# The embedding gate's matrix product by seven block products over both token halves

## The chip, the cores and the metric

The kernel runs on one core of a Trainium2 chip. The metric is the device time of one execution in microseconds (us); the time before is the median of three runs. Beside it stands one profiled execution, from which all rows come. The engines are TensorE (PE, with PEld for its weight loads), VectorE (DVE), ScalarE (ACT), GpSimd (POOL), and the queues that start transfers, SP's and GpSimd's.

## The reference, cut to what matters

One decoder layer over 1024 tokens of width 2048, in float32. After the two attention groups the rest of the layer is:

```
h    = h + mixed @ w_out                                   # 2048 x 2048
gate = sigmoid(rmsnorm(h, norm_ple_g) @ w_ple_gate)        # 2048 x 2048
h    = h + gate * (p @ w_ple_proj)                         # 256 x 2048
out  = rmsnorm(h, norm_final_g)
```

where `rmsnorm(h, g)` divides each token's row by the root of its mean square (plus 1e-6) and multiplies by g. Since the division is one factor per token, it can be made after the product with the gate's weights; the kernel does so.

## The kernel before, in words

Everything is held transposed: 128 channels on the partitions, tokens along the free dimension. The 2048 channels are 16 chunks of 128, the tokens two halves of 512; half 1 (the earlier tokens, stored in reverse) is worked through first. Each float32 operand is split into a high part in the matmul's own format and a low part, what is left; a product of two operands is three matmuls (high by high, low by high, high by low). ScalarE makes the high part with a cast, VectorE the low part with a subtraction.

*The plain product* (`unit`) makes two output chunks for one half of the tokens: 4 pieces of weights, 8 input chunks by weight piece and output chunk, three matmuls each, 96 matmuls of 128x512 in all. The weights stream in 512 KB pieces through `wprep`, which casts and subtracts 1024 columns at once. The input projection and the embedding gate are made so; the gate reads its weights twice, once for each half of the tokens.

*The product by seven* (`class Seven`) takes a matrix product in 2 x 2 blocks, and makes it with seven block products instead of eight, in Winograd's form. One side of the blocks is the token half: rows 1 are half 1, rows 2 half 0. The operands of the seven products are A11, A12, A22 and the sums of rows S1 to S4 on one side, and B11, B21, B22 and the differences of weights T1 to T4 on the other. The V and gate columns of the input projection and the output projection are made this way. Each goes in two stages over the contraction: stage one covers eight of the 16 input chunks and stores half sums in DRAM, stage two covers the other eight, reads the half sums and adds them. A product for one pair of output chunks (`product`, L602 and on) is 4 chunks x 3 = 12 matmuls; an output pair is called u, from 0 to 7. Around each product, `prod` makes one high part (`whigh`) and one low part (`wlow`) of the weights three products ahead, and takes up to two pieces of other work from the queue `xq`, such as the splits of the next stage's operands. The table PLACE says which buffers hold the operands, WRING which buffers the weights' parts go through. A block's buffers come free when its last product of the stage is done; the loads of the next stage's operands are issued then and its splits two products later.

In the output projection (`op = Seven(...)`) the sums of rows S1 to S4 aren't made by VectorE: the attention writes and accumulates them in DRAM (`comb_d`) by transfers while it runs. Stage one writes half sums to `half_d` with plain stores; stage two adds them and accumulates the result by transfers into `h_d`, which holds x beforehand (`put`). At the end of stage two, `gate_loads` reads half 1's sixteen chunks of h back, scales them by `norm_ple_g` and splits them for the gate.

*The gate* then goes half by half. For half 1: eight units over the chunks of h; beside them the chunks of h are loaded once more (`load_h`), squared by ScalarE and summed by GpSimd (`SumSq`), which gives each token's mean square and its root after the third unit. `ple` makes the embedding's product (twelve matmuls for two output chunks), whose result ScalarE copies out of PSUM. `gated` multiplies the accumulator by the root, takes the sigmoid, multiplies by the embedding's product, adds to h, and squares the new h for the last norm. Half 0 follows in the same way, with its own loads, sums and splits. The last output pair of half 0 is made in two quarters of 256 tokens (`for tq`), each followed by the last norm (`final`) and the stores of the output.

The order on TensorE is the order written in the program throughout. In the output projection, and up to the gate's first two units, so are VectorE's and ScalarE's (`man2`); elsewhere a planner sets the order of those, and that of GpSimd and SP everywhere. On every engine instructions run strictly in their order.

## Time and profile before

| | us |
|---|---|
| median of the runs | 2490.62 (2489.23 to 2491.97, three runs) |
| the profiled execution | 2490.54 |
| its span | 2488.8 |
| TensorE busy | 2413.1 |
| VectorE busy | 1810.9 |
| ScalarE busy | 1201.2 |
| GpSimd busy | 280.1 |

The span is the time between the first and the last instruction of the profiled execution. A row of a group names the line of the kernel, the engine, the operation, what it writes and reads, its shapes and its count; behind that stand the busy time, the mean duration of one in ns, and the idle time before it with what ended it. A matmul's duration overlaps the next one's, so the pace is read from starts or from counts, not from durations.

### The profile page before, as it was taken

What the parts mean: (1) busy time and instruction counts of PE and PEld (TensorE: products, weight loads), DVE (VectorE), ACT (ScalarE), POOL (GpSimd) and SP (SyncE); (2) the same over time, 40 slices, a digit from 0 to 9 for tenths busy, and PEclk for the clock granted to TensorE, in tenths of its full rate; (3) what the DMA queues carried; (4) which work ended last, traced back from release to release, by engine and by line L of the source; (5) the groups of instructions that cost most, each with busy time, mean ns of one, the idle gap of its engine ahead of it and who ended that gap; (6) DMA issues with size and microseconds to landing.
All of it is one profiled execution on the core that took longest, in us unless ns stands there. A gap on an engine that the chain in (4) does not pass through costs nothing.

```text
span 2488.8 us, 31941 instructions
## 1 busy us (share of the span) xinstructions
PE 2413.1 (97%) x11434; PEld 2002.3 (80%) x11434; DVE 1810.9 (73%) x3010; ACT 1201.2 (48%) x2063; POOL 280.1 (11%) x361
## 2 busy tenths in 40 slices
PE   8999999999999999999999999998899999999997
PEld 6787878888888887888888888886787887787886
DVE  6788777778877778788888877877678674546555
ACT  5334335555555445565555555445423234546342
POOL 1211110000000000000000001110111113330110
PEclk9999999999999999999999999999999999999998
DMA  8776655444445556334444344555757777343433
GB/s 290 250 271 217 224 171 161 154 146 129 145 143 148 181 158 200 119 110 114 121 117 115 102 127 119 144 153 173 224 167 222 165 192 231 121 129 97 133 109 102
DMA packets 167471, 397.72 MB, mean 160 GB/s; under 512 B 18896, under 2 KB 23248, under 8 KB 167312
## 3 DMA queue, kind: packets, MB, share of 16 engines
q1 hardware_dynamic: 131040, 302.07, 37.7%
q0 software_dynamic: 36272, 93.60, 14.3%
q8 instruction: 90, 1.47, 0.2%
q14 instruction: 69, 0.57, 0.1%
HBM read 297.03 MB, written 106.95 MB: 162 GB/s over the span
## 4 chain that ended last, share of the span: by engine, by line
PE 82%; DVE 8%; DMA 4%; ACT 3%; issue 3%; SPq 0%; DVEq 0%; ACTq 0%
PE acc L232 17%; PE acc L233 17%; PE acc L234 17%; PE pbc L611 4%; PE pbc L609 4%; PE pbc L610 4%; PE tp L407 2%; PE z L311 1%; PE z L310 1%; PE pa L611 1%; PE pa L610 1%; PE pa L609 1%; PE av L454 1%; PE av L453 1%; PE av L452 1%
## 5 line engine op out<-in xcount | busy, mean ns | idle before, releaser
L232 PE MATMUL acc<-xh,whi 128*128 128x512 f32 x1568 | 629.0, 401 | 4.0 <-ACT xh L1070 2.5
L234 PE MATMUL acc<-xh,wlo 128*128 128x512 f32 x1568 | 613.8, 391 | 2.2 <-DVE wlo L154 2.2
L233 PE MATMUL acc<-xl,whi 128*128 128x512 f32 x1568 | 613.3, 391 | 0.3 <-DVE xl L1071 0.3
L154 DVE TENSOR_TENSOR wlo<-wraw,whi 128x1024 fp32r<-128x1024 f32 x252 | 312.1, 1239 | 193.3 <-ACT whi L153 187.6
L153 ACT CAST whi<-wraw 128x1024 fp32r<-128x1024 f32 x252 | 264.7, 1050 | 241.3 <-PE acc L233 214.9
L234 PEld LDWEIGHTS acc<-xh,wlo 128*128 128x128 f32 x1568 | 295.0, 188 | 67.5 <-DVE wlo L154 3.5
L232 PEld LDWEIGHTS acc<-xh,whi 128*128 128x128 f32 x1568 | 295.5, 188 | 59.2 <-ACT xh L1070 2.9
L233 PEld LDWEIGHTS acc<-xl,whi 128*128 128x128 f32 x1568 | 296.1, 189 | 54.8 <-DVE xl L1071 0.6
L699 ACT CAST wpr<-T 128x512 fp32r<-128x512 f32 x128 | 78.0, 621 | 317.3 <-DVE T L657 313.0
L426 ACT CAST awh<-tp 128x256 fp32r<-128x256 f32 (+1 forms) x160 | 80.8, 505 | 155.8 <-PE tp L407 155.8
L362 ACT ACTIVATE et<-z,mx 128x512 f32<-128x512 f32 (+7 forms) x128 | 94.8, 741 | 61.1 <-DVE mx L356 52.7
L115 POOL TENSOR_TENSOR ssq<-ssq,sq 128x512 f32<-128x512 f32 x56 | 83.9, 1500 | 304.5 <-ACT sq L114 253.8
L431 DVE TENSOR_TENSOR awl<-tp,awh 128x256 fp32r<-128x256 f32 (+1 forms) x160 | 92.2, 577 | 32.5 <-ACT awh L426 32.4
L356 DVE TENSOR_REDUCE mx<-z 128x1 f32<-128x512 f32 (+7 forms) x128 | 97.0, 758 | 4.4
L341 DVE TENSOR_TENSOR_SCAN st<-pt 128x511 f32<-128x511 f32 (+3 forms) x64 | 86.6, 1353 | 18.0 <-ACT pt L334 16.3
L713 DVE TENSOR_TENSOR wpr<-T,wpr 128x512 fp32r<-128x512 f32 x128 | 87.6, 685 | 6.4 <-ACT wpr L699 4.5
L609 PE MATMUL pbc<-cS,wpr 128*128 128x512 f32 x224 | 87.4, 390 | 3.2 <-DVE u L1485 1.6
L611 PE MATMUL pbc<-cS,wpr 128*128 128x512 f32 x224 | 87.2, 389 | 0.0
L610 PE MATMUL pbc<-cS,wpr 128*128 128x512 f32 x224 | 87.2, 389 | 0.0
L454 PE MATMUL av<-awl,v 128*128 128x256 f32 x256 | 73.8, 288 | 8.4 <-DVE awl L431 8.4
L334 ACT ACTIVATE pt<-z 128x512 f32<-128x512 f32 (+3 forms) x64 | 41.7, 651 | 78.8 <-DVE z L318 73.2
L232 PE MATMUL acc<-cA11h,whi 128*128 128x512 f32 x192 | 76.1, 396 | 0.0
(401 smaller groups left out, 5345.7 us busy)
## 6 DMA issues: line engine op xcount, KB each, us to landing
wraw<-w_in SPq DMA_DIRECT2D x192, 512.0 KB, 3.6
wraw<-w_gate SPq DMA_DIRECT2D x64, 512.0 KB, 3.6
wraw<-w_out SPq DMA_DIRECT2D x72, 256.0 KB, 3.7
wraw<-w_vg SPq DMA_DIRECT2D x71, 256.0 KB, 4.0
comb_d<-sg POOLq DMA_DIRECT2D x48, 256.0 KB, 7.4
spare<-xT SPq DMA_DIRECT2D x44, 256.0 KB, 4.1
xl<-h_d SPq DMA_DIRECT2D x40, 256.0 KB, 5.2
vghalf_d<-hc POOLq DMA_DIRECT2D x32, 256.0 KB, 4.1
```

Of the source, the lines that this page charges most:

```text
L153: side.later(1, lambda: A.copy(hi[:, o], raw[:, o]))
L154: side.later(side.wlo, lambda: V.tensor_tensor(lo[:, o], raw[:, o], hi[:, o].bitcast(F32), op=ALU.subtract))
L232: T.matmul(acc[c], hi[:, k2, kh, c, :], xh, start=first, stop=False)
L233: T.matmul(acc[c], hi[:, k2, kh, c, :], xl, start=False, stop=False)
L234: T.matmul(acc[c], lo[:, k2, kh, c, :], xh, start=False, stop=last)
L356: V.reduce_max(mx, z[:, vw], axis=AX.X, negate=True)
L362: A.activation(et[:, vw], z[:, vw], AF.Exp, bias=mx[:, 0:1], accum_out=l)
L431: V.tensor_tensor(wl[:, o, :], tp[:, o, :], wh[:, o, :].bitcast(F32), op=ALU.subtract)
L454: T.matmul(av, vv[:, 0, blk % 4, :], wl, start=False, stop=last)
L609: T.matmul(o, wh[:, w], xh, start=start and k == 0, stop=False, skip_group_check=True)
L610: T.matmul(o, wh[:, w], xl, start=False, stop=False, skip_group_check=True)
L611: T.matmul(o, wl[:, w], xh, start=False, stop=k == 3, skip_group_check=True)
```

## The change

The embedding gate becomes a third and fourth stage of the same object `op`, with `w_gate` laid out in blocks as `w_out` is. Its products, `Seven(..., 8, 4)`, run on directly behind the output projection's, with no change of weight streams.

- Stage one of the output projection now accumulates into `h_d` (which holds x); stage two reads `h_d` in place of `half_d`, adds, and stores h with plain stores. Two of its additions go from VectorE to GpSimd.
- In stage two, for each output pair u, ScalarE squares the four new chunks of h and GpSimd adds the squares, in pieces of 256 columns, into one sum for each half. VectorE makes the sums of rows S1 to S4 for the gate, scaled by `norm_ple_g` (`sums`), and SP stores them in `hcomb_d`.
- The gate's first stage (ph = 2) covers input chunks 0 to 3 and 8 to 11, its second (ph = 3) chunks 4 to 7 and 12 to 15. The first loads its operands as the output projection's last products free the buffers. The subtraction of four of these splits is GpSimd's. Both roots are made in the first stage.
- The second stage has only five of the seven products, those that half 1 needs. With them half 1 is finished: embedding product, sigmoid, addition to h, squares. What half 0 needs from them is added up and stored in `q_d`; the weight differences T3 and T4 that half 0 needs are stored in `tw_d`.
- A last pass of two products a unit (S3 by T3, A22 by T4) finishes half 0. In it the last norm of half 1 is made by GpSimd, in products of 1024 columns. Units 6 and 7 of the last pass are made in two quarters of 256 tokens at the end.
- The order of VectorE and ScalarE is the written one up to the end of the last pass's unit 5. `soon` holds steps that run one to three products later; up to three pieces of `xq` are taken behind a product when more than eight wait.

The diff, cut to its core:

```diff
-            def split(self, nm, i, hi, lo, gain=None, raw=None):
+            def split(self, nm, i, hi, lo, gain=None, raw=None, eng=V, apart=False):
...
+                def low():
+                    if gain is None:
+                        eng.tensor_tensor(lo, raw, hi.bitcast(F32), op=ALU.subtract)
+                    else:
+                        V.scalar_tensor_tensor(lo, raw, gain, hi.bitcast(F32), op0=ALU.mult, op1=ALU.subtract)
+                    self.XC[nm, i] = hi, lo
+
+                if apart:
+                    self.soon.append((self.slot + 1, low))
+                else:
+                    low()
...
+            def sources3(self, n, u, b22_):
+                def t2():
+                    self.diff("T1", "awh", self.B[12], self.B[11])
+                    self.wload(n + 1, 11)
+                    return self.diff("T2", "awl", b22_, self.T["T1"])
+                def t1():
+                    nc.sync.dma_start(tw_d[u][:, 0, :], self.diff("T3", "awh", self.B[12], b22_))
+                    self.wload(n + 1, 12)
+                    return self.t1
+                def b22():
+                    nc.sync.dma_start(tw_d[u][:, 1, :], self.diff("T4", "awl", self.B[21], self.T["T2"]))
+                    self.wload(n + 1, 21)
+                    return b22_
...
-                for _ in range(2):
+                for _ in range(3 if len(self.xq) > 8 else 2):
                     if self.xq and self.xq[0][0] <= self.slot:
                         self.xq.popleft()[1]()
...
-        op = Seven(lambda u, ph, k: ap["w_out"][u, ph, k], 8)
+        op = Seven(lambda u, ph, k: ap["w_out" if ph < 2 else "w_gate"][u, ph % 2, k], 8, 4)
+        tw_d = dram.tile([8, P, 2, HALF], F32, name="tw_d", tag="tw_d")
+        hcomb_d = dram.tile([4, 8, P, HALF], F32, name="hcomb_d", tag="hcomb_d")
+        q_d = dram.tile([8, 2, P, HALF], F32, name="q_d", tag="q_d")
...
+        class Squares:
...
+                elif self.wide:
+                    s = ev.tile([P, HALF], F32, name="s", tag="sq", bufs=2)
+                    A.activation(s, t, AF.Square)
+                    G.tensor_tensor(self.acc, self.acc, s, op=ALU.add)
+                else:
+                    for j in range(2):
+                        o = slice(j * 2 * P, j * 2 * P + 2 * P)
+                        s = ev.tile([P, 2 * P], F32, name="s", tag="sm", bufs=5)
+                        A.activation(s, t[:, o], AF.Square)
+                        G.tensor_tensor(self.acc[:, o], self.acc[:, o], s, op=ALU.add)
...
         def put(o, ph, hf, ch):
-            if ph:
+            if ph == 0:
                 G.dma_start(h_d[hf, ch], o, accum_op=ALU.add)
+            elif ph == 1:
+                G.dma_start(h_d[hf, ch], o)
+                ssh[hf].add(o)
             else:
                 G.dma_start(half_d[hf, ch], o)
...
+        def sums(u, hq, a2, b1):
...
+            def one():
+                A.activation(b2, b2, AF.Copy, scale=gb)
+                V.scalar_tensor_tensor(b2, a2, ga, b2, op0=ALU.mult, op1=ALU.add)
+                store("S1", b2)
+                V.tensor_tensor(a2, a2, a1, op=ALU.subtract)
+                store("S3", a2)
+            def two():
+                V.scalar_tensor_tensor(a1, a1, ma, b2, op0=ALU.mult, op1=ALU.add)
+                store("S2", a1)
+                V.scalar_tensor_tensor(b1, b1, mb, a1, op0=ALU.mult, op1=ALU.add)
+                store("S4", b1)
...
+        def gating(half, u, c, o, z):
+            V.tensor_tensor(o, o, rstd[half], op=ALU.mult)
+            def gate():
+                t = hpair[half, u][:, c, :]
+                V.tensor_tensor(o, o, z, op=ALU.mult)
+                V.tensor_tensor(t, t, o, op=ALU.add)
+            def squared():
+                t = hpair[half, u][:, c, :]
+                s2[half].add(t)
+                A.activation(t, t, AF.Copy, scale=gvec[:, 2, u + 8 * c:u + 8 * c + 1])
+            op.soon.extend([(op.slot + 1, lambda: A.activation(o, o, AF.Sigmoid)), (op.slot + 2, gate), (op.slot + 3, squared)])
...
+        begin(0)()
+        for u in range(6):
+            embedded = begin(u + 1) if u < 5 else None
+            prod(u, 4, "A22", bs[u], False)
+            q1, _ = qs.pop(u)
+            V.tensor_tensor(q1, bs[u], q1, op=ALU.add)
+            gating(0, u, 0, q1, zs[u])
+            if embedded:
+                embedded()
...
+            elif u > 2:
+                final(1, slice(0, HALF), s2[1].acc, {3: (4, 5), 4: (6, 7, 0), 5: (1, 2, 3)}[u], G)
...
-    a["w_gate"] = wsq(w_ple_gate)
+    a["w_gate"] = c(w_ple_gate[0].reshape(2, 2, 4, P, 2, 8, P).transpose(5, 1, 0, 3, 4, 2, 6).reshape(8, 2, 2, P, 2, 4 * P))
```

More of the change, by code (lines that the diff above doesn't have):

```diff
@@ L727, in prod @@
                 self.slot += 1
+                if u == 7 and len(self.units) == 32:
+                    for k in range(4):
+                        del self.XC[nm, k]
                 self.whigh()
@@ L1457, in rest_of, with embedding_load @@
             put(o, ph, hf, ch)
-        for ph in range(2):
+            if ph == 1:
+                hrows[u, hf] = o
+                if not first:
+                    xq.extend((op.slot + 1, fn) for fn in sums(u, hq, hrows.pop((u, 0)), hrows.pop((u, 1))))
+        praws = []
+        def embedding_load(half):
+            for k in range(2):
+                praw = ev.tile([P, HALF], F32, name="praw", tag="xt", bufs=4)
+                nc.sync.dma_start(praw, ap["pT"][k * P:(k + 1) * P, half * HALF:half * HALF + HALF])
+                praws.append(praw)
@@ L1499, in _body @@
                         rest_of(prev, False)
[L1500 to L1501 removed]
+                    p2()
                     prod(u, ph, "S1", c, True)
@@ L1651, in _body @@
[L1651 to L1662 removed]
+            b = {}
@@ new lines, in _body @@
+            ms = pp.tile([P, Q], F32, name="ssps", tag="t")
+            T.matmul(ms, ones, s2[0].acc[:, ts], start=True, stop=False)
+            for n, (u, c, o) in enumerate(os):
+                t = hpair[0, u][:, c, ts]
+                V.tensor_tensor(o, o, rstd[0][:, ts], op=ALU.mult)
+                sgi = A.activation(o, o, AF.Sigmoid)
+                V.tensor_tensor(o, o, z[u][:, c, ts], op=ALU.mult)
+                V.tensor_tensor(t, t, o, op=ALU.add)
+                s = ev.tile([P, Q], F32, name="sq", tag="sm", bufs=5)
+                if n < 3:
+                    A.activation(s, t, AF.Square)
+                else:
+                    V.tensor_tensor(s, t, t, op=ALU.mult)
+                T.matmul(ms, ones, s, start=False, stop=n == 3)
```

571 lines of the change are left out of this document (291 added, 280 removed).

## The prediction

> **What bounds the kernel now.** I read the page's busy times first, then the busy time of each engine by stretch, with the stretches laid at the seams between the stages, then what TensorE waited for.
>
> ```profile
> span 2488.8 us, 31941 instructions
> PE 2413.1 (97%) x11434; PEld 2002.3 (80%) x11434; DVE 1810.9 (73%) x3010; ACT 1201.2 (48%) x2063; POOL 280.1 (11%) x361
> ```
> ```profile
> core 0: us, PE busy (x) PEld busy (x) DVE busy (x) ACT busy (x) POOL busy (x), PEclk, DMA share, GB/s
> 1805.98:1898.57 92.59, 92.59 (x410) 76.62 (x408) 66.69 (x106) 26.56 (x47) 10.85 (x20) 1.00 0.55 184
> 1898.57:2051.58 153.01, 150.75 (x661) 123.39 (x660) 112.04 (x177) 46.44 (x83) 25.48 (x31) 1.00 0.76 187
> 2051.58:2071.06 19.48, 16.90 (x73) 13.36 (x72) 13.85 (x21) 9.68 (x16) 3.39 (x4) 1.00 1.01 276
> 2071.06:2258.68 187.62, 186.11 (x819) 153.47 (x818) 91.67 (x101) 99.51 (x140) 63.78 (x43) 1.00 0.44 144
> 2258.68:2300.49 41.81, 37.31 (x142) 27.87 (x140) 20.81 (x28) 22.82 (x29) 0.00 (x0) 0.92 0.32 100
> 2300.49:2447.37 146.88, 146.88 (x650) 121.66 (x649) 77.17 (x80) 58.90 (x79) 17.37 (x11) 1.00 0.36 117
> 2447.37:2489.00 41.63, 26.82 (x205) 25.13 (x203) 22.76 (x45) 11.42 (x18) 2.79 (x2) 0.83 0.31 102
> ```
>
> From the top: the output projection's first pass, its second pass, the seam to the gate, the gate of half 1, the seam between the halves, the gate of half 0, the end. TensorE is busy throughout; VectorE has 112 of 153 us in the second pass and half its time in the gate. So this part is bound by the number of matmuls, as long as the other engines keep up. Two stretches inside steady stages give the pace:
>
> ```profile
> 2300.49:2322.25 21.76, 21.76 (x98) 18.02 (x96) 11.64 (x14) 9.22 (x12) 1.82 (x1) 1.00 0.41 134
> 1939.98:1959.03 19.05, 19.05 (x86) 15.72 (x84) 12.86 (x20) 4.54 (x8) 3.42 (x4) 1.00 0.75 166
> ```
>
> The first is one unit of the gate, 96 weight loads and matmuls in 21.76 us: 0.2267 us per 128x512 matmul (two more matmuls only touch its edges). The second is one unit of the output projection's second pass, seven products of twelve, 2.72 us a product, 19.05 a unit; VectorE spends 20 instructions on it.
>
> **What is removed.** The plain gate takes 16 x 96 = 1536 matmuls of 512 columns (one unit as twice as many of 256). Seven products instead of eight take 1344. 192 x 0.2267 = 43.5 us go from TensorE; the program's order of instructions bears it out (146 fewer of 512 columns, 92 fewer of 256). With the plain gate go its own seams. Counting matmuls against stretches: 72 x 0.2267 = 16.3 of 19.48 us, so 3.2 lost at the seam to the gate; 816 x 0.2267 + 0.5 for the sums = 185.5 of 187.62, 2.1 lost in half 1; 132 x 0.2267 + 2.6 for the sums = 32.5 of 41.81, 9.3 lost between the halves. The waits name them:
>
> ```profile
> PE ple L1329 <- ACT ph L1301: 3.3, 2, 2.9
> PE pbc L609 <- DVE hc L1515: 2.5, 2, 1.8
> PE acc L232 <- DVE gt L1341: 1.5, 1, 1.5
> ```
>
> Together 14.6 us. The new order has no change of halves of that kind: both halves' rows are in each product, and rstd is ready in the gate's first pass. What takes their place is priced below, so I take all 14.6 off.
>
> **What is added, by the unit.** TensorE's order is fixed by hand and so is VectorE's and ScalarE's up to the last pass, so a stage goes at TensorE's pace or at VectorE's, whichever is longer. The durations:
>
> ```profile
> L713 DVE TENSOR_TENSOR wpr<-T,wpr 128x512 fp32r<-128x512 f32 x61 | 41.8, 685 | 0.9
> L115 POOL TENSOR_TENSOR ssq<-ssq,sq 128x512 f32<-128x512 f32 x56 | 83.9, 1500 | 304.5 <-ACT sq L114 253.8 <-ACT ssq L110 48.6
> 2192.20 2.68 POOL L115 TENSOR_TENSOR ssq<-ssq,sq 128x512 f32<-128x512 f32 x2 [7.61 <-ACT sq L114]
> 2145.22 0.68 DVE L1341 TENSOR_TENSOR gt<-zb,rstd 128x512 f32<-128x512 f32 x1
> 2145.82 0.68 DVE L1343 TENSOR_TENSOR gt<-gt,pls 128x512 f32<-128x512 f32 x1
> 2146.42 0.68 DVE L1341 TENSOR_TENSOR gt<-zb,rstd 128x512 f32<-128x512 f32 x1
> 2147.02 1.72 DVE L154 TENSOR_TENSOR wlo<-wraw,whi 128x1024 fp32r<-128x1024 f32 x1
> 2148.67 1.77 DVE L1344 TENSOR_TENSOR h<-h,gt 128x512 f32<-128x512 f32 x1
> 2146.32 3.58 POOL L115 TENSOR_TENSOR ssq<-ssq,sq 128x512 f32<-128x512 f32 x2 [25.11 <-ACT sq L114]
> ```
>
> VectorE's 512-column instructions start 0.60 us apart, so 0.61 each. GpSimd's addition of 512 columns takes 1.29 undisturbed (2.68 for two), 1.50 on average. The last rows are the dear ones: while GpSimd adds, VectorE's L1341, which reads one operand from PSUM, keeps 0.68, but L154 and L1344, both operands in SBUF, stretch, L1344 from 0.68 to 1.77. GpSimd's time is thus VectorE's time whenever VectorE's next instruction reads two operands from SBUF. The change raises GpSimd's additions from 56 of 512 columns to 47 of 512, 90 of 256 and 8 of 1024. For 256 I take half of 1.29, 0.65 (bounds: 0.65, and 1.29 if width did not matter); for 1024 twice, 2.58 (bounds 1.29 and 3.58).
>
> Output projection, second pass: 22 VectorE instructions (two additions go to GpSimd, four sums of rows come) = 13.4 us, GpSimd 2 x 1.29 + 8 x 0.65 = 7.8. Six of the 22 read PSUM, so 27% of GpSimd's time is covered: 13.4 + 0.73 x 7.8 = 19.1 against 19.05. At the edge: 0 to (13.4 + 7.8 - 19.05) x 8 = 17; I take 3 for unevenness.
>
> Seam to the gate: in two units VectorE issues 66 instructions (24 splits, eight sums among them), 40.3 us, and GpSimd 15.5 (four splits, twelve squares' additions, two others), 0.73 of it exposed: 51.6 against 2 x 19.05 = 38.1. 13.5 late; weights are prepared three products ahead, 8.2 us of lead. Lost 5.3 if the lead is whole, 13.5 if the pass before has eaten it: 9. The transfers crowd too: 28 operands, four rows, sums and weights are some 15 MB in 17 products (46 us), 326 GB/s, and today's seam in its fullest five, with the DMA share at 0.99, moved 327:
>
> ```profile
> 2045.00:2050.00 5.00, 5.00 (x24) 4.13 (x23) 4.91 (x8) 1.38 (x4) 0.84 (x1) 1.00 0.99 327
> ```
>
> They run beside the VectorE queue that is late anyhow; if not hidden, they alone would cost up to 5.
>
> Gate, first pass: 17 instructions, 10.4 of 19.05 us, GpSimd nearly idle: 0. Seam to its second pass: 36 instructions, 22.0 against 19.05, inside the lead: 1 (0 to 3). Second pass: five products and twelve embedding matmuls, 16.3 us a unit; 21 instructions, 12.8, and GpSimd 5.2, 71% exposed: 16.5. Eight units: 1.6, bounds 0 and (18.0 - 16.3) x 8 = 13.6; 2. Entry of the last pass: 33 instructions, 20.1 + 3.7 against 19.0, 4.8 late with some 3.7 of lead left: 3 (1 to 5).
>
> Last pass: two products and twelve embedding matmuls, 8.16 a unit; 11 instructions (6.7) and two additions at 64% (1.7) make 8.4. Into its second half fall the eight 1024-column products of half 1's norm, which were VectorE's: 8 x 2.58 = 20.6, 64% of it 13.2. Bounds 0 and 20; 10, a little slack taken off.
>
> The end. Today the last gate matmul starts at 2471.55 and VectorE's two quarters of the output are apart, the first under matmuls:
>
> ```profile
> 2471.55 0.28 PE L1650 MATMUL acq<-xh,wz 128*128 128x256 f32 x1
> 2479.16 4.30 DVE L1264 TENSOR_TENSOR h<-h,r 128x512 f32<-128x512 f32 x7
> 2483.38 0.87 DVE L1261 SCALAR_TENSOR_TENSOR h<-h,gvec,r 128x256 f32<-128x256 f32 x2
> 2468.30 16.57 SPq L1271 DMA_DIRECT2D out_dram<-h  x16
> ```
>
> In the new order both quarters stand behind the last matmul, and one more addition does: 5.2 more, covered in part by the second root's chain: 5 (0 to 10).
>
> TensorE's clock: after its longest wait (2.85) the matmuls started 0.43 apart for some microseconds, then 0.23 again, and that seam's row has the clock at 0.92; the seam to the gate, with waits up to 1.8, has it at 1.00.
>
> ```profile
> 2264.41 0.49 PE L1329 MATMUL ple<-ph,pwh 128*128 128x512 f32 x1 [2.85 <-ACT ph L1301]
> ```
> ```profile
> 2269.00 0.43 PE ple L1329
> 2273.97 0.23 PE acc L234
> ```
>
> The new stalls come in bits; one stretch of the first kind costs 0.08 x 41.8 = 3.3, none 0: I take 2. The Trainium skill (TensorE: Matmul & The Clock Gate, "What's actually happening") says the clock falls only after an idle window of about 3.4 us. By that the clock's term would be 0 and the sum 2 lower; the trace, with 2.9 us as its longest wait there and 0.43 behind it, is the harsher of the two.
>
> Costed at nothing, with their cover:
>
> ```profile
> L699 ACT CAST wpr<-T 128x512 fp32r<-128x512 f32 x61 | 37.3, 621 | 169.1 <-DVE T L657 169.1
> L1368 POOL DMA_DIRECT2D h_d<-hc x32 | 27.2, 852 | 123.0 <-DVE hc L1456 56.9 <-DVE hc L1515 47.6 <-DVE hc L1494 14.7
> L1370 POOL DMA_DIRECT2D half_d<-hc x25 | 13.6, 543 | 112.7 <-DVE hc L1456 72.8 <-DVE hc L1515 33.3 <-DVE wpr L713 5.2
> ```
>
> ScalarE has nine instructions of 0.62 and eight half as wide in a unit of the second pass, 9 of 19 us. The accumulating stores move from the second pass to the first: 32 x (0.85 - 0.54) = 10 us of GpSimd's issuing, into a stretch where it is busy 11 of 93 us and the DMA share is 0.55; uncovered, those 10 would be the price. SP's queue gets 140 more issues; a stored weight difference waits there for VectorE ahead of the next weight's load, covered by the three products of lead, and a bit of the 9 and 2 above if the lead is gone. Preparing the gate's weights twice in 1024-column pieces becomes preparing them once in 512-column pieces and differences; these are in the instruction counts above.
>
> Sum: 3 + 9 + 1 + 2 + 3 + 10 + 5 + 2 = 35 us of new losses. The profiled run took 2490.54, its span 2488.8, the median of the runs shown 2490.62, so one scale serves. 2490.5 - 43.5 - 14.6 + 35 = **2467.4**.
>
> **Rivals.** *Cover holds*: GpSimd's pieces fall into VectorE's gaps and the lead swallows the seams. For it: VectorE had 41 us free in the second pass. Against it: it has 5.6 of 19 us free now, and GpSimd wants 7.8. Left are the end (5), the entry (1), the seam (5) and unevenness (3): 2490.5 - 58.1 + 14 = 2446.
>
> *GpSimd takes VectorE's place as the bound* (the other side): nothing runs beside GpSimd's additions, because VectorE's queue nearly always has an instruction with two SBUF operands in front. Second pass 17, seam 13.5, 1024-column products 20, gate's second pass 13.6, entry 5, end 10, clock 3.3, gate's seam 3: 85, so 2490.5 - 58.1 + 85 = 2517. It decides from 58 us of losses on, that is when about 60% of the covered time isn't covered. For it L1344's 1.77; against it L1341's 0.68. The Trainium skill (SBUF — State Buffer, "Who interferes with whom") has this as an exclusive lock: whoever starts first keeps it for the whole instruction and the other blocks, and an instruction with at most one SBUF input is exempt. By that rule the trace's two kinds of rows are as they must be, and the six exempt instructions of 22 are all the cover there is.
>
> *The gain goes to transfers*, and the change doesn't do what it says: on top of the 35, 5 at each of three seams, and 1 in each of the last pass's six units, whose 1.8 MB in 8.16 us are 220 GB/s: 56, so 2488. For it the 0.99 above; against it the gate's 0.36 to 0.44.
>
> **How the numbers follow.** The forecast 0.50 (2452 to 2483), cover holds 0.23, GpSimd as the bound 0.18 (2497 to 2517), transfers 0.09 (five of the nine within 0.2%). A measurement of this kernel tells about 0.2%, 5 us, from no change. Faster: 0.50 + 0.23 + 0.04 = 0.77; same 0.06; slower 0.17. Range 2441 to 2504: below it a tenth, above it a tenth.
>
> **What would show it.** Gate matmuls still 0.2267 apart, a product 2.72. In the second pass, units of 19 to 20 us with VectorE near 95% busy, its two-operand rows averaging about 1.0 instead of 0.69 and waits of TensorE on `wpr`. At the seam a wait of TensorE of 5 to 13 us in all. In the last pass the eight 1024-column rows on GpSimd near 2.6 and VectorE's additions beside them above 2. I am wrong if VectorE's rows stay at 0.69 beside GpSimd, if units run over 21 us, or if TensorE waits for transfers rather than for VectorE.

## The result: 20 us slower

The changed kernel takes 2510.32 us (2510.15 to 2512.22), the kernel before 2490.91 beside it: a ratio of 1.008, with a 95% interval of 1.0063 to 1.0098. The prediction was 2467.4 with a range of 2441 to 2504. The profiled execution took 2510.15, its span 2508.4.

The head of the page of the changed kernel:

```profile
span 2508.4 us, 32433 instructions
PE 2390.8 (95%) x11198; PEld 1970.0 (79%) x11198; DVE 1965.9 (78%) x3251; ACT 1216.6 (48%) x2195; POOL 394.6 (16%) x498
```

TensorE has 22 us less busy time, GpSimd 115 and VectorE 155 more. The busy time of each engine by stretch, the stretches laid where TensorE starts a new pass (columns as in the prediction's table):

```profile
1906.84:2073.82 166.98, 159.04 (x673) 124.13 (x672) 140.75 (x189) 72.13 (x151) 87.12 (x101) 1.00 0.69 223
2073.82:2127.78 53.96, 44.68 (x169) 34.62 (x168) 46.62 (x61) 25.04 (x47) 19.24 (x20) 0.87 0.62 215
2127.78:2243.82 116.04, 116.04 (x509) 95.38 (x508) 72.64 (x112) 40.89 (x71) 12.96 (x24) 1.00 0.43 142
2243.82:2386.34 142.52, 136.41 (x589) 110.51 (x587) 126.54 (x177) 67.82 (x128) 53.29 (x58) 0.99 0.76 251
2386.34:2401.05 14.71, 10.27 (x39) 8.01 (x37) 14.61 (x22) 7.91 (x15) 4.25 (x5) 0.88 1.04 393
2401.05:2461.63 60.58, 47.61 (x195) 37.28 (x194) 57.16 (x59) 35.09 (x55) 35.91 (x19) 0.94 0.57 199
2461.63:2508.40 46.77, 27.54 (x140) 22.92 (x140) 34.74 (x73) 16.66 (x32) 5.49 (x4) 0.77 0.28 90
```

From the top: the output projection's second pass, the two units of the seam to the gate, the rest of the gate's first pass, its second pass, the entry of the last pass, the last pass, the two quarters with the end. What a stretch would take at TensorE's pace is the matmuls that the program has in it, by 0.2267 us (two of 256 columns count as one); what is above that is lost. Three rows are set beside the kernel before. It started the second pass at 1898.57; it took 153.0 us for 660 matmuls in that pass (149.6 at TensorE's pace, 3.4 lost); and it took 41.4 us, from 2447.37 on, for 96 matmuls and the end (21.8, 19.7 lost).

| stretch | taken | at TensorE's pace | lost | lost more than before | predicted (bounds) |
|---|---|---|---|---|---|
| up to the second pass | | | | 8.3 | 0 |
| second pass, 672 matmuls | 167.0 | 152.4 | 14.6 | 11.2 | 3 (0 to 17) |
| seam, 168 | 54.0 | 38.1 | 15.9 | 15.9 | 9 (5.3 to 13.5) |
| rest of the gate's first pass, 504 | 116.0 | 114.3 | 1.7 (two sums of squares) | 1.7 | 0 |
| gate's second pass, 587 | 142.5 | 133.1 | 9.4 | 9.4 | 1 + 2 (0 to 16.6) |
| entry of the last pass, 37 | 14.7 | 8.4 | 6.3 | 6.3 | 3 (1 to 5) |
| last pass, 192 and a sum of 1.1 | 60.6 | 44.6 | 16.0 | 16.0 | 10 (0 to 20) |
| the quarters and the end, 72 | 46.8 | 16.3 | 30.4 | 10.8 | 5 (0 to 10) |
| clock | | | | some 10, in the rows | 2 (0 to 3.3) |

The new losses add up to 79.6, against 35 in the prediction. The sums of squares that stand in no loss became 2.0 shorter (3.1 before, 1.1 now), so 2490.5 - 58.1 - 2.0 + 79.6 = 2510.0, and the profiled run took 2510.15. The saving of 58.1 thus came as reckoned, and the miss of 42.9 lies in the losses. What TensorE waited for from the second pass on, the four largest:

```profile
PE pa L616 <- DVE wpr L764: 13.5, 8, 4.4
PE pb L614 <- DVE qt L1749: 10.1, 3, 6.3
PE pbc L616 <- DVE wpr L764: 4.7, 7, 0.8
PE pbc L614 <- DVE hc L1683: 4.4, 1, 4.4
```

All four are VectorE: the weights' low parts (`wpr`) and accumulators it had not yet read. The next are shorter, among them 3.1 us for ScalarE's squares at the end and 2.4 for its casts of weights in the second pass. A steady unit of the second pass, and VectorE's own waits in it:

```profile
1967.37:1988.62 21.25, 20.09 (x85) 15.45 (x84) 17.12 (x23) 7.73 (x18) 11.74 (x15) 1.00 0.60 197
```
```profile
DVE wpr L764 <- ACT wpr L750: 1.5, 2, 0.8
DVE hc L1479 <- PE pbc L616: 1.4, 1, 1.4
DVE u L1551 <- PE pbc L616: 0.9, 1, 0.9
DVE hq L1458 <- ACT hq L1457: 0.8, 1, 0.8
```

The unit takes 21.25 in place of 19.05, and yet VectorE is busy for 17.12 of it only. It isn't full: it waits 4.6 us for TensorE and ScalarE, and TensorE then waits for it (0.8 us, and 0.4 for a cast that itself waits for VectorE). In the last pass GpSimd's rows and VectorE's beside them:

```profile
2433.00 22.36 POOL L1719 TENSOR_TENSOR h<-h,s2t 128x1024 f32<-128x1024 f32 x8
```
```profile
2436.33 0.68 DVE L1729 TENSOR_TENSOR qt<-pb,qt 128x512 f32<-128x512 f32 x1
2437.04 2.18 DVE L1618 TENSOR_TENSOR qt<-qt,ssh 128x512 f32<-128x512 f32 x1
2439.14 2.84 DVE L764 TENSOR_TENSOR wpr<-wraw,wpr 128x512 fp32r<-128x512 f32 x1
2441.90 0.68 DVE L1622 TENSOR_TENSOR qt<-qt,ple 128x512 f32<-128x512 f32 x1
```

With an operand in PSUM (`pb`, `ple`) an instruction keeps 0.68; with both in SBUF it takes 2.18 and 2.84, about the length of one of GpSimd's products (22.36 / 8 = 2.8).

### The profile page after: what moved, and what is told of

Read it like the earlier page. It is cut to its first block, busy times and chain, and to the rows that moved or that the text cites. A ratio compares the mean times of both kernels' runs of the same rounds, so it can differ in the third digit from the quotient of the medians.

```text
span 2508.4 us, 32433 instructions
## 1 busy us (share of the span) xinstructions
PE 2390.8 (95%) x11198; PEld 1970.0 (79%) x11198; DVE 1965.9 (78%) x3251; ACT 1216.6 (48%) x2195; POOL 394.6 (16%) x498
## 5 line engine op out<-in xcount | busy, mean ns | idle before, releaser
L227 PE MATMUL acc<-xh,whi 128*128 128x512 f32 x1152 | 466.2, 405 | 2.5 <-ACT xh L1136 2.5
L229 PE MATMUL acc<-xh,wlo 128*128 128x512 f32 x1152 | 452.3, 393 | 2.2 <-DVE wlo L154 2.2
L228 PE MATMUL acc<-xl,whi 128*128 128x512 f32 x1152 | 451.5, 392 | 0.3 <-DVE xl L1137 0.3
L154 DVE TENSOR_TENSOR wlo<-wraw,whi 128x1024 fp32r<-128x1024 f32 x192 | 234.1, 1220 | 48.5 <-ACT whi L153 47.1
L229 PEld LDWEIGHTS acc<-xh,wlo 128*128 128x128 f32 x1152 | 216.8, 188 | 51.2 <-DVE wlo L154 3.5
L227 PEld LDWEIGHTS acc<-xh,whi 128*128 128x128 f32 x1152 | 217.5, 189 | 40.7 <-ACT xh L1136 2.9
L228 PEld LDWEIGHTS acc<-xl,whi 128*128 128x128 f32 x1152 | 217.9, 189 | 38.1 <-DVE xl L1137 0.6
L614 PE MATMUL pbc<-cS,wpr 128*128 128x512 f32 x320 | 124.8, 390 | 3.2 <-DVE u L1551 1.6
L616 PE MATMUL pbc<-cS,wpr 128*128 128x512 f32 x320 | 124.5, 389 | 0.0
L615 PE MATMUL pbc<-cS,wpr 128*128 128x512 f32 x320 | 124.5, 389 | 0.0
L764 DVE TENSOR_TENSOR wpr<-wraw,wpr 128x512 fp32r<-128x512 f32 x80 | 77.3, 966 | 11.5 <-ACT wpr L750 11.5
L616 PE MATMUL pbc<-cS2h,wpr 128*128 128x512 f32 x176 | 71.8, 408 | 7.3 <-DVE wpr L764 7.3
```

Of the source, the lines that this page charges most:

```text
L154: side.later(side.wlo, lambda: V.tensor_tensor(lo[:, o], raw[:, o], hi[:, o].bitcast(F32), op=ALU.subtract))
L227: T.matmul(acc[c], hi[:, k2, kh, c, :], xh, start=first, stop=False)
L228: T.matmul(acc[c], hi[:, k2, kh, c, :], xl, start=False, stop=False)
L229: T.matmul(acc[c], lo[:, k2, kh, c, :], xh, start=False, stop=last)
L614: T.matmul(o, wh[:, w], xh, start=start and k == 0, stop=False, skip_group_check=True)
L615: T.matmul(o, wh[:, w], xl, start=False, stop=False, skip_group_check=True)
```

## The experiments

The theory going in: GpSimd's arithmetic on SBUF holds up VectorE's instructions with two SBUF operands, and through them TensorE. Unless another is named, the base is the changed kernel, 2510.32. The numbers in brackets are ratios to the kernel before with their 95% interval; the changed kernel's is 1.0063 to 1.0098, and the interval of an edit worth 5 us still touches it, so that such a difference is known to some 2 us.

### GpSimd's additions of the squares (second pass)

Left out (`adds` is False for the output projection's squares):

```diff
-                        G.tensor_tensor(self.acc[:, o], self.acc[:, o], s, op=ALU.add)
+                        if self.adds:
+                            G.tensor_tensor(self.acc[:, o], self.acc[:, o], s, op=ALU.add)
```

> The changed kernel, with GpSimd's additions of the squares in the output projection's second pass left out (92 or so of 256 columns; ScalarE still makes the squares, so the gate's root comes from one chunk alone and the numbers are wrong). Theory (GpSimd's additions hold up VectorE's instructions with two SBUF operands): the units of the second pass go from 21.25 us to 19.1 to 19.6, the pass from 167 to 155 or less, the seam to the gate gets 2 to 5 us shorter, and the whole 2510 comes to 2492 to 2498. Rival one (ScalarE's squares stand ahead of the weights' casts in its queue, and that chain is late): units of 20.7 or more, 2505 to 2510. Rival two (VectorE's own 22 instructions a unit, or the transfers, are the bound): no change, 2508 to 2512.

Given to VectorE:

```diff
+                        else:
+                            op.soon.append((op.slot + 1, partial(V.tensor_tensor, self.acc[:, o], self.acc[:, o], s, op=ALU.add)))
```

> The changed kernel, with the same additions of squares made by VectorE one product later in place of GpSimd: eight more instructions of 256 columns a unit on the engine that TensorE waits for. Theory (GpSimd's additions block VectorE): VectorE's unit is 13.4 + 8 x 0.4 = 16.6 us of unstretched work, under 19.05, so most of the gain of leaving the additions out stays: units of 19.3 to 20, the whole 2494 to 2503. Rival (VectorE's own instructions are the bound): each unit gets longer by the 3.2 us added, the whole 2520 to 2535.

Measured: 2490.88 without them (ratio to before 1.0005, 0.9994 to 1.0015), 2495.60 with VectorE making them (1.0020, 1.0010 to 1.0029). One unit, first without, then with them on VectorE:

```profile
1963.80:1982.97 19.17, 19.17 (x85) 15.71 (x84) 14.88 (x23) 7.74 (x18) 5.48 (x6) 1.00 0.67 220
```
```profile
1963.46:1982.81 19.35, 19.35 (x85) 15.63 (x84) 17.36 (x31) 7.74 (x18) 5.49 (x6) 1.00 0.66 215
```

The second pass comes from 167.0 to 154.1 and 155.2, the seam from 54.0 to 50.2 and 51.8. So the theory holds, and both rivals fall: ScalarE's squares are all still there, and more instructions on VectorE made the unit shorter. The three units say more than that. VectorE is busy 17.12 us with the additions on GpSimd and 17.36 with them on its own queue, and TensorE loses 2.2 us in the one and 0.3 in the other. It is not the amount of VectorE's time that GpSimd takes (17.12 - 14.88 = 2.2 of its 6.3 us of additions) but where it takes it: the first two rows below are the changed kernel's unit at its start, GpSimd's additions and VectorE's low part, for which TensorE waits; the third is the same instruction when VectorE makes the additions.

```profile
1966.86 1.43 POOL L1353 TENSOR_TENSOR ssh<-ssh,s 128x256 f32<-128x256 f32 x2
```
```profile
1967.35 1.50 DVE L764 TENSOR_TENSOR wpr<-wraw,wpr 128x512 fp32r<-128x512 f32 x1 [0.76 <-ACT wpr L750]
```
```profile
1963.13 0.69 DVE L764 TENSOR_TENSOR wpr<-wraw,wpr 128x512 fp32r<-128x512 f32 x1
```

TensorE's other wait in this unit goes back to GpSimd as well. Beside the next additions (from 1971.86) a difference of weights takes 1.94 in place of 0.69, ScalarE's cast waits for it, and TensorE for the cast:

```profile
1971.91 1.94 DVE L664 TENSOR_TENSOR T<-b,T 128x512 f32<-128x512 f32 x1
```
```profile
1973.89 0.62 ACT L750 CAST wpr<-T 128x512 fp32r<-128x512 f32 x1 [2.16 <-DVE T L664]
```
```profile
1974.56 0.50 PE L614 MATMUL pbc<-cS2h,wpr 128*128 128x512 f32 x1 [0.35 <-ACT wpr L750]
```

On VectorE's queue the additions stand behind the weights' low part and fill its waits; on GpSimd they run whenever a square is ready, and stretch what happens to be in front. The Trainium skill (SBUF — State Buffer, "Who interferes with whom") says that a VectorE instruction with at most one SBUF input, outside of the two-port modes, doesn't contend with GpSimd, and that issue order decides who blocks. The rows with 0.68 and 2.84 above agree with the first; no run here turns the order of issue alone around.

### All of GpSimd's arithmetic up to the last pass given to VectorE

```diff
-            return partial(op.split, nm, i, hi, lo, gain, None, G if ph == 2 and nm in ("S1", "S4") and i < 2 else V, ph > 0)
+            return partial(op.split, nm, i, hi, lo, gain, None, V, ph > 0)
```

> The changed kernel, with the four splits of the gate's first operands that GpSimd makes given to VectorE. Theory (GpSimd's SBUF work stretches VectorE's at the seam to the gate): VectorE does four more at 0.61, 2.4 us, and is freed of about two thirds of GpSimd's 7.6 us (2110 and 1719 ns each), so the seam gets 2 to 3 us shorter, the whole 2507 to 2509. Rival one (VectorE's count of instructions alone bounds the seam): 2.4 us longer, 2512 to 2514. Rival two (the transfers bound it): no change, within 1 us of 2510.

```diff
-                    G.tensor_tensor(u2, u2, r[1, u + 8], op=ALU.add)
+                    V.tensor_tensor(u2, u2, r[1, u + 8], op=ALU.add)
...   (s1, q1 and q2 likewise, all squares' additions, and the splits as above)
```

> The changed kernel, with every arithmetic instruction of GpSimd up to the last pass given to VectorE: the squares' additions one product later, the additions of half sums, the sums for half 0 and the four splits. Theory (GpSimd costs VectorE more than its work is worth): units of the output projection's second pass 19.05 to 19.5, the seam 2 us shorter, units of the gate's second pass 16.3 to 16.7 in place of 17.45, so 2510 less 15, 2.5 and 5: 2485 to 2490, at or a little under the kernel before. Rival (VectorE is then the bound itself, with 13.4 + 1.2 + 3.2 = 17.8 us of instructions in a unit of 19.05 and about 15.6 in one of 16.3, and no room for unevenness): units of 20 and 17.5, 2497 to 2508.

Measured: 2508.76 for the splits alone (inside the range expected, but with a seam of 54.8, no shorter), 2496.39 for all (1.0023, 1.0015 to 1.0031). No gain over the squares alone: units of 19.56, seven units of the gate's second pass 122.1 in place of 123.9. The second theory fails here, and its rival is nearer. VectorE was now busy 18.29 of 19.56 in a unit:

```profile
1968.72:1988.28 19.56, 19.44 (x85) 15.61 (x84) 18.29 (x33) 7.74 (x18) 2.16 (x4) 1.00 0.65 213
```

So giving work back paid while VectorE had waits to fill; with 18.29 of 19.56 it gained nothing more.

### The seam: VectorE or the transfers

Ten low parts left out (`skip` is true in the gate's first pass for the last two chunks of A11, S2, A12, S1 and S4):

```diff
                 def low():
-                    if gain is None:
+                    if skip:
+                        pass
+                    elif gain is None:
```

> The changed kernel, with ten of VectorE's low-part subtractions at the seam to the gate left out (the last two chunks of A11, S2, A12, S1 and S4; the matmuls then read the unsplit row as its own low part, so the numbers are wrong; transfers, casts and matmuls stay). Theory (the seam is bound by VectorE's count of instructions, whoever else reads SBUF): ten at 0.7 us go, and the two units of the seam come from 54 us to 47 to 49, the whole 2503 to 2505. Rival (the transfers bound it, their share is 0.9 to 1.0 there at some 320 GB/s): no change, 2509 to 2511.

Measured: 2505.61 (1.0058, 1.0043 to 1.0073), the seam 48.1. The first of its two units, in the changed kernel and with the ten left out:

```profile
2073.82:2101.31 27.49, 22.64 (x85) 17.19 (x83) 27.28 (x35) 16.64 (x33) 13.37 (x14) 0.88 0.80 278
```
```profile
2075.31:2098.60 23.29, 21.25 (x86) 16.75 (x84) 23.12 (x29) 16.83 (x33) 13.03 (x14) 0.93 0.93 340
```

VectorE is busy from end to end in both, and the unit is as much shorter as its busy time; the transfers, moving 340 GB/s in place of 278, had had room. So in the first unit it is VectorE's count, as the theory had it. In the second VectorE is busy for 19.33 of 26.47; TensorE's one long wait there, 4.4 us, is again for a low part, which stands behind two splits that take 3.43 beside two of GpSimd's (3.40). TensorE's waits for low parts are 9.0 of the seam's 15.9. Most of the rest is the clock, 0.87 in its row: behind each of the two long waits some twelve matmuls start 0.43 us apart in place of 0.23, 5 us in all. The first of them:

```profile
2078.62 0.80 PE L616 MATMUL pa<-cA11h,wpr 128*128 128x512 f32 x1 [4.18 <-DVE wpr L764]
2079.21 0.63 PE L614 MATMUL pa<-cA11h,wpr 128*128 128x512 f32 x1
2079.64 0.63 PE L615 MATMUL pa<-cA11l,wpr 128*128 128x512 f32 x1
```

So it is after all four waits over 4 us (4.18, 4.43, 4.44, 6.32). After one of 2.62 in the last pass the matmuls kept their pace, but after one of 2.45 at the entry to the gate's second pass they did not:

```profile
2430.62 0.50 PE L614 MATMUL pb<-cS3h,wpr 128*128 128x512 f32 x1 [2.62 <-DVE qt L1749]
2430.95 0.40 PE L615 MATMUL pb<-cS3l,wpr 128*128 128x512 f32 x1
2431.19 0.39 PE L616 MATMUL pb<-cS3h,wpr 128*128 128x512 f32 x1
```
```profile
2251.88 0.80 PE L614 MATMUL pbc<-cA,wpr 128*128 128x512 f32 x1 [2.45 <-DVE hc L1479]
2252.47 0.63 PE L615 MATMUL pbc<-cA,wpr 128*128 128x512 f32 x1
2252.89 0.63 PE L616 MATMUL pbc<-cA,wpr 128*128 128x512 f32 x1
```

The same wait (2.45 and 2.46) was followed by some five matmuls at full pace and then 0.43 in the run without the squares' additions, and by full pace throughout in the version put together below. Over the five places of the changed kernel, up to the end of the last pass, the slow matmuls cost some 10 us. The Trainium skill (TensorE: Matmul & The Clock Gate, "What's actually happening") puts the fall behind an idle window of about 3.4 us. The waits over 4 us and the one of 2.62 agree with it; the 2.45 does not, nor does the 2.85 of the kernel before, shown in the prediction, where three waits under 1 us came between it and the 0.43. What decides between 2.4 and 2.9 us, no run here shows.

### The last pass

Half 1's norm on VectorE, and left out on either:

```diff
-                final(1, slice(0, HALF), s2[1].acc, {3: (4, 5), 4: (6, 7, 0), 5: (1, 2, 3)}[u], G)
+                final(1, slice(0, HALF), s2[1].acc, {3: (4, 5), 4: (6, 7, 0), 5: (1, 2, 3)}[u], V)
```

> The changed kernel, with the eight products of 1024 columns that make half 1's last norm given back to VectorE. Theory (they block VectorE's SBUF instructions for most of their 22.6 us): VectorE's own eight take some 1.2 us each, 9.6 in all, against 22.6 x 0.64 = 14 blocked, so the last pass gets 4 to 8 us shorter, the whole 2502 to 2506. Rival (GpSimd's products run beside VectorE's work and the last pass is late by VectorE's own instructions): the 9.6 us are added, less a little slack, 2514 to 2520.

```diff
-                    eng.tensor_tensor(t, t, r.unsqueeze(1).to_broadcast([P, 2, ts.stop - ts.start]), op=ALU.mult)
+                    if half == 0:
+                        eng.tensor_tensor(t, t, r.unsqueeze(1).to_broadcast([P, 2, ts.stop - ts.start]), op=ALU.mult)
```

> The changed kernel, with the eight products of 1024 columns of half 1's last norm left out (its rows are stored without the factor, the transfers stay). It gives the whole price of those products in the last pass, which came out the same on either engine. Theory (on GpSimd they block VectorE for most of their 22.6 us): the last pass is 10 to 14 us shorter, the whole 2496 to 2500. Rival (the last pass is late by VectorE's own order, a chain through the sigmoid and the weights' casts, and the products fill its gaps): 0 to 4 us, 2506 to 2510.

The squares' additions left out as well:

```diff
-                    G.tensor_tensor(self.acc, self.acc, s, op=ALU.add)
+                    if not self.wide:
+                        G.tensor_tensor(self.acc, self.acc, s, op=ALU.add)
```

> As the run before it, and GpSimd's additions of half 0's squares in the last pass left out too (its last norm is then made from one chunk's squares), so that GpSimd does no arithmetic behind the last pass's entry. Theory: the units of the last pass come down to 8.16 to 8.5 us and only the entry's loss is left, the whole 3 to 6 us below the run before it, 2491 to 2496. Rival (VectorE's own instructions bound the pass): units of 9 or more and no further gain, within 2 us of the run before it.

Measured: 2510.84 on VectorE, 2505.52 without the norm (1.0059, 1.0046 to 1.0072), 2497.09 without both (1.0031, 1.0021 to 1.0040). With the norm on VectorE the whole did not change, though the last pass itself came to 55.7 in place of 60.6: the end took 51.6 in place of 46.8. The rows stretched by GpSimd's products were gone, but the products stood two or three in a row ahead of the weights, and VectorE once waited 3.6 us behind them for a load of h; six of the eight products now stood in the end's stretch. Without the norm the pass took 56.1; the whole fell by 4.8, between the theory's 10 to 14 and the rival's 0 to 4. Left out after it, the eleven 512-column additions gave more than the eight products of twice the width, 8.4 us against the 3 to 6 expected: 4.9 in the pass (51.2 left) and most of the rest at the end. The units didn't come down to the 8.5 expected. 51.2 is still 6.6 above TensorE's pace without any of GpSimd's arithmetic, so 9.4 of the 16.0 lost went with GpSimd's. What shows in the rest is a late transfer: ScalarE's cast of a weight difference waits for it, and VectorE waits 4.3 us behind the casts (that run's order of time on ScalarE, and VectorE's waits from 2400 to 2451):

```profile
2411.30 0.62 ACT L750 CAST wpr<-wraw 128x512 fp32r<-128x512 f32 x1 [6.99 <-DMA wraw<-tw_d]
```
```profile
DVE pwhl L1517 <- ACT pwhl L1516: 4.9, 2, 4.3
```

### Transfers at the entry of the last pass

```diff
-                qs[u + 2] = load_q(u + 2)
+                with tc.issue_after(q1i.ins): qs[u + 2] = load_q(u + 2)
```

> The changed kernel, with the last pass's loads of half 0's stored sums held back until the unit two before has been added up, in place of running ahead as buffers allow (same transfers, same order). Theory (at the entry of the last pass, where the transfers move 390 GB/s for 35 us, ScalarE's and VectorE's queues wait for weights behind these loads: 5.35 us for tw_d, 3.2 for w_pp): those waits shrink by half, the last pass is 2 to 4 us shorter, the whole 2506 to 2508. Rival (the waits are hidden by what VectorE is late with anyway): within 1 us of 2510.

```diff
-                kt = PLACE["A12" if u < 4 else "S4"][u % 4][1]
+                kt = PLACE["A12"][u % 3][1]
```

> The changed kernel, with the buffers for half 0's stored sums cut from sixteen to six (three units), so that their loads wait for a buffer and are spread over the last pass; the hold tried before had not moved a single load. Theory (at the entry of the last pass the weights' transfers stand behind these loads): ScalarE's wait of 5.35 us for tw_d falls under 3, the last pass is 2 to 4 us shorter, the whole 2506 to 2508. Rival (what is late there is VectorE and the chain of two weight buffers): within 1 us of 2510.

The first edit moved no load (seven of them were issued in a row at 2396, as without it), so its 2510.50 tells nothing of transfers; it repeats the changed kernel, with every stage the same within 0.7 us. The second gave 2507.09 (1.0063, 1.0050 to 1.0076): ScalarE's wait for `tw_d` went from 7.2 in all to 0.4, its wait for the embedding's weights from 3.2 to 5.1, and the last pass with its entry got 1.1 shorter, the end 2.2. None of its four runs is as slow as one of the unedited kernel's, but the intervals overlap. Some 1 to 3 us may be the transfers'; that isn't settled.

### The accumulating stores

```diff
-                G.dma_start(h_d[hf, ch], o, accum_op=ALU.add)
+                G.dma_start(h_d[hf, ch], o)
```

> The changed kernel, with the first pass's stores into h_d made plain in place of accumulating (the residual x is left out of the result, nothing else changes: same transfers, same queue, same order). The second pass starts at 1906.8 after the change, at 1898.6 before it. Theory (the accumulating stores, moved to the first pass, cost those 8 us, by GpSimd's issuing and by reading back what they add to): the second pass starts 5 to 8 us earlier, the whole 2502 to 2506. Rival (the 8 us come from the order of loads at the end of attention or of the added ones, not from these stores): less than 2 us, 2508 to 2512.

The same part alone, in the kernel before:

```diff
             if ph:
-                G.dma_start(h_d[hf, ch], o, accum_op=ALU.add)
+                G.dma_start(h_d[hf, ch], o)
             else:
-                G.dma_start(half_d[hf, ch], o)
+                G.dma_start(h_d[hf, ch], o, accum_op=ALU.add)
...
-                    nc.sync.dma_start(r[e], half_d[e])
+                    nc.sync.dma_start(r[e], h_d[e])
```

> The kernel before, with one part of the change alone: the output projection's first pass accumulates into h_d and its second pass reads that back, adds and stores plainly (same result, same number of transfers). Theory (the accumulating stores at the end of attention and in the first pass are what the first pass lost): the second pass starts 4 to 7 us later than the 1898.6 of the kernel before, the whole 2494 to 2498. Rival (they hide there as the prediction had it, GpSimd's issuing only): within 2 us of 2491.

Only the eight stores made while attention runs, plain:

```diff
-                put(o, 0, 1, u + i)
+                G.dma_start(h_d[1, u + i], o)
```

> The changed kernel, with only the eight stores into h_d made while attention still runs plain, the other 24 of the first pass accumulating as in the change (x is missing from these eight chunks). Theory (the accumulating stores cost at the seam into the first pass, where the transfers' share is 1.0): most of the 5.7 us that all 32 gave come back, 2505 to 2507. Rival (the cost lies in the steady first pass, by the 24): less than 1.5 us, 2508.5 to 2511.

Measured: 2504.62 with all plain (5.7 less than the changed kernel; 1.0063, 1.0046 to 1.0080), 2496.14 for the kernel before with that part alone (5.7 more than the 2490.44 beside it; 1.0023, 1.0013 to 1.0032), 2504.99 with the eight plain (5.3 less; 1.0054, 1.0037 to 1.0070). Undone and done alone, the part costs the same, and the eight at the end of attention are nearly all of it. The second pass started at 1898.2 with all plain and at 1901.1 with the eight plain, in place of 1906.8. From the third of the eight stores to the first store of the pass itself it took 50.5 us in both kernels that accumulate them, and 47.0 to 47.4 in the three that store them plainly. The stretch around the seam into the first pass, in the kernel before, then in the changed one, then with the eight plain:

```profile
1780.00:1800.00 20.00, 17.24 (x78) 13.72 (x76) 9.15 (x15) 6.77 (x13) 3.78 (x5) 1.00 0.94 299
```
```profile
1780.00:1800.00 20.00, 17.32 (x83) 14.15 (x82) 9.79 (x15) 8.15 (x15) 5.21 (x6) 1.00 1.01 258
```
```profile
1780.00:1800.00 20.00, 18.41 (x85) 15.00 (x84) 9.12 (x15) 6.62 (x13) 4.33 (x6) 1.00 0.98 298
```

There the transfers are nearly full in each (0.94 to 1.01), and with accumulating stores they moved 258 GB/s in place of 299. The two other runs fit, if less sharply: 278 GB/s with all stores plain, 257 in the kernel before with the part alone. In the steady first pass the share rises too, from 0.52 in the kernel before to 0.79, at the same rate:

```profile
1820.00:1860.00 40.00, 40.00 (x178) 33.15 (x177) 29.77 (x48) 11.17 (x20) 4.42 (x9) 1.00 0.52 176
```
```profile
1820.00:1860.00 40.00, 40.00 (x177) 32.82 (x176) 28.23 (x46) 10.75 (x20) 7.73 (x9) 1.00 0.79 178
```

but there is room, and TensorE is busy throughout: the other 24 stores cost nothing to speak of.

### A version put together from these

The output projection's squares are added by VectorE; half 0's squares are summed by TensorE into a PSUM bank; half 1's norm is made by VectorE, one product at a time (the core of the edit; the loads of the stored sums are held back too, which alone had moved nothing):

```diff
-                    G.tensor_tensor(self.acc, self.acc, s, op=ALU.add)
+                    op.soon.append((op.slot + 2, partial(T.matmul, self.acc, onesr, s, start=self.wide == 1, stop=False, skip_group_check=True)))
...
-                final(1, slice(0, HALF), s2[1].acc, {3: (4, 5), 4: (6, 7, 0), 5: (1, 2, 3)}[u], G)
+                for n, v in enumerate({2: (4,), 3: (5, 6), 4: (7, 0), 5: (1, 2, 3)}[u]):
+                    op.soon.append((op.slot + n + 1, partial(final, 1, slice(0, HALF), s2[1].acc, (v,))))
```

> The changed kernel put together from what the runs point to: the squares' additions of the output projection on VectorE (2495.6 alone), the squares of half 0 in the last pass summed by TensorE into a PSUM bank (twelve matmuls, 2.7 us, in place of GpSimd's eleven additions, whose removal gave 8), half 1's norm on VectorE one product at a time, the stored sums' loads held back. Theory: 2484 to 2490, under the kernel before. Rival (VectorE's eleven instructions a unit and the norm's 9.6 us are the last pass's bound whatever GpSimd does): 2493 to 2499.

> The version put together before (2485.0 against the 2490.4 of the kernel before), with the hold that moved nothing taken out and the buffers of the stored sums cut to six as in the first run of this batch. Theory (transfers at the last pass's entry cost): 2 us or more below, 2480 to 2483. Rival: the same as that version, 2484 to 2487.

Measured: 2484.97 (ratio to before 0.9975, 0.9967 to 0.9984), and 2485.62 with the six buffers (0.9980, 0.9970 to 0.9990), no further gain. The first is 25 us below the changed kernel and 5.5 below the kernel before: the seven products do pay, by a quarter of a per cent, once most of GpSimd's arithmetic is taken from beside VectorE.

## Why the prediction was wrong

**What held.** Matmuls at 0.2267 and products of 2.72; the saving of 58.1 (the sum closes to 0.2 us); the rest of the gate's first pass at TensorE's pace, but for two sums of squares; the length of the 1024-column products, 2.8 for 2.58, and VectorE's rows beside them above 2. Of the signs that it named for being wrong, one came: units over 21 us.

**The step that failed first** is the one on which each stage was reckoned: "a stage goes at TensorE's pace or at VectorE's, whichever is longer". By it the second pass lost next to nothing, 19.1 against 19.05 in a unit, and 3 for unevenness. VectorE was never full in a steady unit (17.12 of 21.25), nor did GpSimd's additions of the squares take as much from it as was put down (2.2 us of a unit, not 0.73 x 5.2 = 3.8). But the queues in written order wait for each other in a circle: VectorE for accumulators and casts, ScalarE's casts for VectorE's differences, TensorE for low parts and casts. A stretch at the wrong place becomes TensorE's wait although VectorE has 4 us free in the unit. The loss of 14.6 lies inside the bounds, but by luck: the upper bound of 17 was meant for GpSimd with nothing beside it. The same goes for the rival that carries it ("GpSimd takes VectorE's place as the bound", 2517), which came within 7 us: VectorE was not full in the second pass, its 20 for the wide products came out near 4.5, and it had nothing for the stores.

**The stores costed at nothing.** The cover was named as the first pass, with its share of 0.55. It did cover what lay there. The eight stores that leave earlier, at the end of attention, meet a share of 0.94, and that place was not looked at: 5.3 of the 8.3 lost before the second pass. The remaining 3 are within what the start of this pass moves from run to run (1905 to 1909.5 with the stores as changed).

**Terms that were mis-sized.** The clock, given 2 for all stages together, cost some 10: five waits of 2.45 to 6.32 us each brought half pace. The seam, 15.9 for 9 plus the clock: TensorE's waits for low parts were 9.0, in the first unit by VectorE's count as put down, and the clock 5. The last pass, 16.0 for 10: GpSimd's part is 9.4, as much of it by the narrow additions (4.9) as by the wide products (4.5), which had been given 13.2; 6.6 are left without GpSimd, beside a late transfer whose own price isn't settled. The quarters and the end, 10.8 for 5: some 4 of it went with GpSimd's additions of the squares. The entry, 6.3 for 3, is a wait of 4.4 for an accumulator and the slow matmuls behind it, with VectorE busy for 14.61 of the 14.71 us. The gate's second pass, 9.4 for 3, stayed inside its bounds; 4 of it are the wait of 2.45 at its entry and the slow matmuls behind it, giving VectorE GpSimd's sums changed little (122.1 for 123.9), and what limits the rest is not shown.

**The other rivals.** Transfers: shown at the end of attention, not at the seam to the gate, open at the entry of the last pass. Cover holds: no.

## What to carry to other kernels

Don't price a helper engine by the sum of busy times: ask which instruction of the engine that TensorE waits for stands beside it, and who waits for that instruction. Work can be cheaper on that engine, as long as its queue has waits to fill and the work is placed behind the urgent instruction, than on an idle engine that picks its own moment. And when stores change their kind, look at the transfers' share at each place where they leave, the fullest above all, not at the stage they mostly belong to.

## What was not expected of the hardware

An accumulating store loads the transfer queues far more than its bytes say: at the same 176 to 178 GB/s the share went from 0.52 to 0.79, and where the share was already nearly full the rate was 257 and 258 GB/s with them, 278 to 299 with plain ones. And VectorE's eight additions of 256 columns cost it 17.36 - 14.88 = 2.5 us a unit, about as much as it lost (2.2) to GpSimd's making them. Nor does the length of a wait alone tell whether TensorE's clock falls: behind 2.45 us it did, behind 2.62 it did not.
